# A hybrid attention and expert layer: the first norm's gain and bias applied after the turn, the residual rows made later, the first pair's small products moved

## The chip, the core and the metric

The kernel runs on one core of a Trainium2 chip. Five engines work side by side, each through its own queue in order: PE (TensorE, matrix products), DVE (VectorE), ACT (ScalarE), POOL (GpSimd) and SP (SyncE, which here only issues DMAs). Data move between memory and the core's SBUF by 16 DMA engines. The metric is the device time of one execution in microseconds, as the median of several runs.

## What is computed

One layer on 512 tokens of width 1024, in float32: a layer norm, two kinds of attention from one input projection, an output projection with a residual, a second norm, 32 experts of which each token uses two, and a last norm.

```python
h = layer_norm(x, ln_emb_g, ln_emb_b)
proj = h @ w_in[l]
qa, ka, va, cq, ckv, kr = jnp.split(proj, IN_SPLITS, axis=-1)
...
mixed = jnp.concatenate([rms_norm(out_a, ...), rms_norm(out_b, ...)], -1) @ w_out[l]
h = layer_norm(DEEPNORM_ALPHA * h + mixed, ln_attn_g[l], ln_attn_b[l])
ffn = hierarchical_moe(h, ...)      # group, then top 2 of 8 experts; silu(t@gate)*(t@up) @ down
h = layer_norm(DEEPNORM_ALPHA * h + ffn, ln_ffn_g[l], ln_ffn_b[l])
```

So the first norm's result is used twice: turned (features on partitions) as the operand of `w_in`, and as rows (tokens on partitions) in the residual sum before the second norm.

## The kernel before

Tokens are in four tiles of 128. **First norm.** For each tile `load_x` brings `xt`; `ln_stats` forms mean and 1/deviation on DVE (with a power on POOL); `layer_norm` writes the row tile `z[t]` with two DVE instructions for each half of 512, from the gain and bias `lng` and `lnb` that stand broadcast on all partitions. PE turns `z[t]` in eight 128x128 pieces into the PSUM tile `ptr`, and `split` makes of it `hth` (rounded, on ACT) and `htl` (the rest, on DVE), since every product is made of three: high by high, low by high, high by low.

**Projection.** `w_in` is worked through in four chunks of at most 512 columns. `chunk_load` loads four pieces `wf` of 512 KB each (four buffers) and splits them into `wh` (ACT) and `wl` (POOL in the first chunk, DVE afterwards). `chunk` makes the products of each token tile in one of four PSUM accumulators (two `pwo`, two `pmm`, in turn). The first and second chunks give the low-rank tokens `cqt`, which are turned and split to `cth` and `ctl`; the third gives the key and value (`kar`, `ka`, `kall`), the fourth the queries of the windowed attention, which go through `rope` (`rp`, then `cqt`, `qa`) and are turned. In these parts a scheduler decides the order on each engine from its own forecast, so the order of the code isn't that of the queues.

**Later parts.** The low-rank projections and both attentions follow. From `manual_schedule` on (L1075) the order of the code is the order of each queue. There the last token tile's output projection is made in halves (`wout_h`, `wout_l`, `add_z`), with the routing of the last two tiles (a and b) between: `logits`, `biased`, `route` (a chain of some ten small DVE instructions), `count` (PE), `place` and `sel0_` (DVE), and the second norm's rows (`norm_gain`, `norm_bias`, `scaled`, `gain`, `shift`). `gather` collects the rows of the first two experts into `xT0`.

**Experts.** 32 experts go in 16 pairs: `gates` (product with the gate and up weights, tile `p_gu`), `gated` (`hid` on ACT and DVE, turned to `hidT`), `down`, `leave_rows` (weighting on DVE, scatter by POOL). Six slots of weights form a ring: a pair's `load_next` issues, on SP's queue, the weight loads of the pair three later as its gates let go of the slots. The first two slots' gate weights are in three pieces: for j = 0 and 1, for j = 2 and 3, for j = 4 to 7 (j counts the 128-row blocks of the token width). Rows of later experts come by `fetch`, an indirect DMA from POOL into `xg`, after `places_rows` has turned 16 small products into row numbers. Pair 0 differs: its gates are cut after j = 1 for these 16 products (`run_pair`), and `residual(0)` scales its rows before the weighting.

## Time and profile before

| | |
|---|---|
| median of three runs | 592.02 us (591.60 to 595.59) |
| the profiled execution's own time | 591.33 us |
| its span | 589.5 us |
| PE busy | 523.4 us, 89% of the span |
| DVE, ACT, POOL busy | 322.6, 222.1, 99.9 us |
| moved by DMA | 141.76 MB |

The span is what the profiler saw from the first instruction to the last; the execution's own time is 1.8 us longer. Busy shares are means over very different stages, so the prediction reads windows of the span, and inside them the order of time.

### The profile page before, as it was taken

Reading aid. Unit: us, or ns where it says so; the run is one execution under the profiler, and the core shown is the slowest. Engines: PE = TensorE matmul, PEld = TensorE weight load, DVE = VectorE, ACT = ScalarE, POOL = GpSimd, SP = SyncE. Lnnn points to the kernel's source line nnn. Section 1 sums busy time; section 2 is a strip of 40 time slices with the busy share of each in tenths; the row PEclk is TensorE's granted clock in tenths of the full one; section 3 lists DMA queues with packets and bytes.
Section 4 is the critical chain, followed back from the end, with each engine's and each line's share of the span. In section 5 each row is a group of like instructions: output and inputs, shape, how many; then the busy total and the mean of one; then the engine's idle time right before and its main releaser. Section 6 shows DMA issues by size and latency. Waiting matters only on the chain. (4 is left out here: it accounts for less than half of the span.)

```text
span 589.5 us, 8004 instructions
## 1 busy us (share of the span) xinstructions
PE 523.4 (89%) x2756; PEld 331.8 (56%) x2757; DVE 322.6 (55%) x882; ACT 222.1 (38%) x477; POOL 99.9 (17%) x141
## 2 busy tenths in 40 slices
PE   2899999999898999999998899999998699979860
PEld 1688898789766777677777444343433234323230
DVE  4946463775688757947768734434524222202177
ACT  2256451564597738856731312111111111101032
POOL 1700221311100000213200201123111101000051
PEclk9999999999899999999999989999999889989985
DMA  8983310221201005991266799999999999999663
GB/s 279 280 290 81 102 43 0 59 81 42 85 16 58 1 1 212 289 367 39 66 258 259 280 391 410 420 415 415 411 417 400 421 418 391 412 420 416 264 267 142
DMA packets 46268, 141.76 MB, mean 240 GB/s; under 512 B 12380, under 2 KB 19420, under 8 KB 37009
## 3 DMA queue, kind: packets, MB, share of 16 engines
q1 hardware_dynamic: 40608, 131.06, 58.5%
q0 software_dynamic: 4464, 8.06, 3.6%
q10 hardware_dynamic: 1152, 2.10, 0.9%
q8 instruction: 23, 0.38, 0.3%
q14 instruction: 21, 0.16, 0.1%
HBM read 133.14 MB, written 16.25 MB: 253 GB/s over the span
## 5 line engine op out<-in xcount | busy, mean ns | idle before, releaser
L1243 PE MATMUL p_gu<-w_gu,xT 128*64 128x512 f32 x512 | 125.0, 613 | 15.0 <-DMA w_gu<-in_w_gu 14.1
L1243 PEld LDWEIGHTS p_gu<-w_gu,xT 128*64 128x64 f32 x512 | 39.6, 141 | 95.6 <-issue 70.0
L1247 ACT ACTIVATE hid<-p_gu 128x256 f32<-128x256 f32 x16 | 6.1, 384 | 176.0 <-PE p_gu L1243 163.9
L1248 DVE TENSOR_TENSOR hid<-hid,p_gu 128x256 f32<-128x256 f32 x16 | 6.7, 421 | 113.9 <-ACT hid L1247 113.8
L1263 PE MATMUL p_y<-w_dn,hidT 128*64 128x512 f32 x256 | 59.9, 611 | 1.0 <-issue 0.6
L1276 DVE SCALAR_TENSOR_TENSOR xg<-p_y,wsl,xg 128x512 f32<-128x512 f32 x30 | 22.5, 751 | 28.4 <-PE p_y L1263 26.5
L1263 PEld LDWEIGHTS p_y<-w_dn,hidT 128*64 128x64 f32 x256 | 17.5, 140 | 31.4 <-issue 29.3
L604 PE MATMUL ptr<-cst,pr 128*128 128x128 f32 x208 | 33.3, 278 | 1.9 <-ACT pr L562 1.4
L1034 POOL DMA_INDIRECT xg<-norm_rows,tok x16 | 16.5, 1032 | 104.5 <-PE p_y L1263 16.8
L1269 POOL DMA_INDIRECT moe_rows<-xg,idx x15 | 15.6, 1039 | 95.0 <-DVE xg L1276 69.6
L604 PEld LDWEIGHTS ptr<-cst,pr 128*128 128x128 f32 x208 | 24.9, 145 | 9.5 <-ACT pr L562 3.2
L577 ACT ACTIVATE pr<-pmm,bnm 128x512 f32<-128x512 f32 x32 | 22.0, 689 | 10.6 <-DVE bnm L574 9.7
L574 DVE TENSOR_REDUCE bnm<-pmm 128x1 f32<-128x512 f32 x32 | 21.9, 687 | 5.3 <-PE pmm L215 4.8
L215 PE MATMUL pmm<-wh,htl 128*128 128x512 f32 (+1 forms) x64 | 24.0, 374 | 0.0
L213 PE MATMUL pmm<-wh,hth 128*128 128x512 f32 (+1 forms) x64 | 23.8, 372 | 0.0
L214 PE MATMUL pmm<-wl,hth 128*128 128x512 f32 (+1 forms) x64 | 23.5, 368 | 0.0
L562 ACT ACTIVATE pr<-pr,rc 128x512 f32<-128x512 f32 (+2 forms) x32 | 20.6, 645 | 4.1 <-DVE rc L560 3.9
L590 DVE CUSTOM_DVE_ANT_0 sm<-pmm,mask,nsink 128x256 f32<-128x256 f32 (+1 forms) x32 | 17.4, 545 | 7.6 <-PE pmm L587 6.5
L215 PE MATMUL pwo<-wh,htl 128*128 128x512 f32 (+1 forms) x56 | 20.7, 370 | 0.0
L214 PE MATMUL pwo<-wl,hth 128*128 128x512 f32 (+1 forms) x56 | 20.5, 367 | 0.0
L213 PE MATMUL pwo<-wh,hth 128*128 128x512 f32 (+1 forms) x56 | 20.5, 367 | 0.0
L1232 ACT ACTIVATE xg<-xg,of 128x1024 f32<-128x1024 f32 x15 | 17.2, 1149 | 8.5 <-PE p_x L1228 7.8
(349 smaller groups left out, 1161.6 us busy)
## 6 DMA issues: line engine op xcount, KB each, us to landing
w_gu<-in_w_gu SPq DMA_DIRECT2D x52, 1024.0 KB
w_dn<-in_w_dn SPq DMA_DIRECT2D x20, 1024.0 KB
w_gu<-in_w_gu SPq DMA_DIRECT2D x24, 512.0 KB
w_dn<-in_w_dn SPq DMA_DIRECT2D x24, 512.0 KB
wf<-in_w_in SPq DMA_DIRECT2D x12, 512.0 KB
moe_rows<-zr SPq DMA_DIRECT2D x8, 512.0 KB
rows<-moe_rows SPq DMA_DIRECT2D x8, 512.0 KB
wf<-in_w_q_b SPq DMA_DIRECT2D x12, 192.0 KB
```

The source lines that it names most:

```text
L213: PE.matmul(ps, ah, bh, start=first, stop=False)
L214: PE.matmul(ps, ah, bl, start=False, stop=False)
L215: PE.matmul(ps, al, bh, start=False, stop=last)
L562: SC.mul(pr[:, :n], pr[:, :n], rc)
L574: V.tensor_reduce(nm, sp, AX.X, ALU.max, negate=True)
L577: exps_.append(SC.activation(pr[:, :S], sp, AF.Exp, bias=nm, accum_out=den).ins)
L590: V.tensor_tensor_reduce(sm[:, :nk], sp[:, :nk], mask[:, mo:mo + nk], 1.0, nsink[:, h:h + 1], ALU.add, ALU.min, nm)
L604: PE.transpose(pt[:, k * P:(k + 1) * P], pr[:, k * P:(k + 1) * P], ident)
L1232: SC.mul(pl["xg"], pl["xg"], pl["of"])
L1243: PE.matmul(pg[64 * i:64 * i + 64], xT[:, j, 64 * i:64 * i + 64], ws[i][0][j], start=(j == 0), stop=(j == 7))
L1263: r = PE.matmul(py[64 * i:64 * i + 64, :], hT[:, j, 64 * i:64 * i + 64], ws[i][1][n][:, j], start=(j == 0), stop=(j == 1))
L1276: V.scalar_tensor_tensor(y, py, pl["wsl"], y, ALU.mult, ALU.add)
```

## The change

1. **First norm.** The four broadcast loads of `lng` and `lnb` (256 KB each) go, and so do the 16 DVE instructions of `layer_norm`. `cst` (identity and tables) is loaded first and by ACT's queue, with a new small tile `geT` that holds gain and bias with features on partitions (given by the host). ACT now writes z = x * rs + nb in two instructions for each tile; the turned pieces get gain and bias as per-partition numbers on their way from `ptr` into a new SBUF tile `hf`, six by DVE and two by ACT for each token tile; `split` reads `hf`. The first chunk's `wl` is split by DVE like the others.
2. **Residual rows.** `z` now lacks gain and bias. They are loaded, broadcast, into two of the fourth chunk's `wf` buffers (512 KB each), and 16 DVE instructions of 128x512 apply them, in the code inside the fourth chunk's loop.
3. **Last routing.** `logits(a)` is made inside `wout_h(0)`, `route(a)` goes ahead of `place(0)`, `count(a)` behind `turn(b, 1)`, and some norm steps change places.
4. **First pair.** The gates of pair 0 run without a cut in the order j = 4 to 7, 0 to 3; the 16 small products go into `gated`'s two gaps (`rows_mm`), so that the fetches, `residual(0)` and `places_mm` come after them; `weights(1..3)` is called ahead of the gates, and the fetches of pair 1's rows are issued in the order 1, 0, 2, 3.

DVE from the program's first loads on, before (z_64 and z_65 are the rows of the first two token tiles):

```order
L192 BN_STATS ln_st<-xt 128x6 x2
L194 BN_AGGR ln_mv<-ln_st 128x2
L181 TENSOR_SCALAR rsq_t<-ln_mv 128x1
L203 SCALAR_TENSOR_TENSOR z_64<-xt,ln_mv,lng 128x512
L204 SCALAR_TENSOR_TENSOR z_64<-z_64,ln_rs,lnb 128x512
L203 SCALAR_TENSOR_TENSOR z_64<-xt,ln_mv,lng 128x512
L348 CAST identr<-cst 128x128
L204 SCALAR_TENSOR_TENSOR z_64<-z_64,ln_rs,lnb 128x512
L209 TENSOR_TENSOR htl<-ptr,hth 128x4x128
L192 BN_STATS ln_st<-xt 128x6 x2
L209 TENSOR_TENSOR htl<-ptr,hth 128x4x128
```

and now:

```order
L191 BN_STATS ln_st<-xt 128x6
L351 CAST identr<-cst 128x128
L191 BN_STATS ln_st<-xt 128x6
L193 BN_AGGR ln_mv<-ln_st 128x2
L180 TENSOR_SCALAR rsq_t<-ln_mv 128x1
L248 SCALAR_TENSOR_TENSOR ln_nb_156<-ln_mv,ln_rs 128x1
L191 BN_STATS ln_st<-xt 128x6
L201 TENSOR_TENSOR wl<-wf,wh 128x1024
L191 BN_STATS ln_st<-xt 128x6
L262 TENSOR_SCALAR hf<-ptr,geT 128x128 x4
L193 BN_AGGR ln_mv<-ln_st 128x2
L262 TENSOR_SCALAR hf<-ptr,geT 128x128
```

The writing of `z` is gone from DVE, and the weight splits and the `hf` instructions have come between the statistics and the first `htl`.

DVE where the third chunk ends and the fourth begins, before (rp_990 belongs to the first query tile):

```order
L424 TENSOR_TENSOR ka_922<-kar,ka_922 128x256
L431 CAST kall<-ptr 128x2x128 x2
L321 TENSOR_TENSOR rp_990<-pwo,ctq 128x512
L329 TENSOR_TENSOR rp_991<-pwo,stq 128x8x32 x2
L209 TENSOR_TENSOR qa_996<-cqt,qa_996 128x8x64
L321 TENSOR_TENSOR rp_1037<-pmm,ctq 128x512
```

and now (wf is the tile that holds the gain, then the bias):

```order
L427 TENSOR_TENSOR ka_958<-kar,ka_958 128x256
L447 TENSOR_TENSOR z_64<-z_64,wf 128x512 x2
L447 TENSOR_TENSOR z_65<-z_65,wf 128x512 x2
L447 TENSOR_TENSOR z_66<-z_66,wf 128x512 x2
L447 TENSOR_TENSOR z_67<-z_67,wf 128x512 x2
L434 CAST kall<-ptr 128x2x128
L448 TENSOR_TENSOR z_64<-z_64,wf 128x512 x2
L448 TENSOR_TENSOR z_65<-z_65,wf 128x512 x2
L448 TENSOR_TENSOR z_66<-z_66,wf 128x512 x2
L448 TENSOR_TENSOR z_67<-z_67,wf 128x512
L434 CAST kall<-ptr 128x2x128
L448 TENSOR_TENSOR z_67<-z_67,wf 128x512
```

The scheduler has put all 16 row instructions in one block ahead of the first query tile's `rope`, around the last two key casts.

PE in pair 0, before, from the second half of the gates for j = 1 on (w_gu_2878 and w_gu_2884 are the two experts' pieces for j = 0 and 1; psd takes the small products):

```order
L1243 MATMUL p_gu<-w_gu_2878,xT 64x512
L1243 MATMUL p_gu<-w_gu_2884,xT 64x512
L1368 MATMUL psd<-cmb_73,sel_2562 128x2 x2
L1368 MATMUL psd<-cmb_73,sel 128x2 x2
L1368 MATMUL psd<-cmb_74,sel 128x2 x4
L1368 MATMUL psd<-cmb_75,sel 128x2 x4
L1368 MATMUL psd<-cmb_76,sel 128x2 x4
L1243 MATMUL p_gu<-w_gu_2880,xT 64x512
```

and now, from the last gates on (the pieces for j = 2 and 3; those for j = 4 to 7, then 0 and 1, stand ahead of them):

```order
L1254 MATMUL p_gu<-w_gu_2942,xT 64x512
L1254 MATMUL p_gu<-w_gu_2936,xT 64x512
L1254 MATMUL p_gu<-w_gu_2942,xT 64x512
L1391 MATMUL psd<-cmb_73,sel_2618 128x2 x2
L1391 MATMUL psd<-cmb_73,sel 128x2 x2
L1391 MATMUL psd<-cmb_74,sel 128x2 x4
L1263 MATMUL p_t<-cst,hid 128x128 x2
L1391 MATMUL psd<-cmb_75,sel 128x2 x4
L1391 MATMUL psd<-cmb_76,sel 128x2 x4
L1007 MATMUL p_i<-cmb_73,sel_2618 128x6 x2
```

The 16 small products have left the middle of the gates and stand on both sides of the turn of `hid` (`p_t`), with `places_mm` (`p_i`) behind.

```diff
@@ -137,12 +137,11 @@
             t = pl.tile([P, n], F32, name=name)
             SY.dma_start(out=t, in_=src.partition_broadcast(P))
             return t
+
+        geT = cp.tile([P, 2, NK], F32, name="geT")
+        SC.dma_start(out=cst, in_=A["cst"][:, :C_KEEP])
+        SC.dma_start(out=geT, in_=A["ge_T"])
         load_x(0)
-        lg, lb = [lp.tile([P, D], F32, name=nm) for nm in ("lng", "lnb")]
-        for n in range(2):
-            for dst, nm in ((lg, "ln_emb_g"), (lb, "ln_emb_b")):
-                SY.dma_start(out=dst[:, 512 * n:512 * n + 512], in_=A[nm][512 * n:512 * n + 512].partition_broadcast(P))
-        SY.dma_start(out=cst, in_=A["cst"][:, :C_KEEP])
 
         nch = [-1]
 
@@ -162,7 +161,7 @@
                                  in_=A["w_in"][0, 256 * q:256 * q + 256, c0:c0 + w]
                                  .rearrange("(k p) f -> p k f", p=P))
                     o += w
-                split(wf[:, :, :n], wh[:, :, :n], wl[:, :, :n], PO if nch[0] == 0 else V)
+                split(wf[:, :, :n], wh[:, :, :n], wl[:, :, :n])
                 hs.append((wh, wl))
             return n, hs
 
@@ -196,13 +195,6 @@
             rsqrt(rs, mv[:, 1:2], 1.0, eps)
             return mv, rs
 
-        def layer_norm(src, dst, g, b):
-            mv, rs = ln_stats(src)
-            for i in range(2):
-                sl = slice(512 * i, 512 * i + 512)
-                V.scalar_tensor_tensor(dst[:, sl], src[:, sl], mv[:, 0:1], g[:, sl], ALU.subtract, ALU.mult)
-                V.scalar_tensor_tensor(dst[:, sl], dst[:, sl], rs, b[:, sl], ALU.mult, ALU.add)
-
         def split(src, hi, lo, ev=None):
 
             r = SC.copy(hi, src).ins
@@ -250,15 +242,26 @@
                 chunks.append(chunk_load([(768, 512)]))
             elif t + 1 < NT:
                 load_x(t + 1)
-            layer_norm(xs[t], z[t], lg, lb)
+
+            mv, rs = ln_stats(xs[t])
+            nb = small.tile([P, 1], F32, name="ln_nb0")
+            V.scalar_tensor_tensor(nb, mv[:, 0:1], -1.0, rs, ALU.mult, ALU.mult)
             for kk in range(2):
+                sl = slice(512 * kk, 512 * kk + 512)
+                SC.activation(z[t][:, sl], xs[t][:, sl], AF.Identity, scale=rs, bias=nb)
                 pt = ptr()
                 for k in range(4):
                     PE.transpose(pt[:, k * P:(k + 1) * P],
                                  z[t][:, (4 * kk + k) * P:(4 * kk + k + 1) * P], ident)
-                pv = pt.rearrange("p (a b) -> p a b", a=4)
+                hf = lp.tile([P, 4, P], F32, name="hf", bufs=2)
+                for k in range(4):
+                    g_, b_ = [geT[:, i, 4 * kk + k:4 * kk + k + 1] for i in range(2)]
+                    if kk and k % 2:
+                        SC.activation(hf[:, k], pt[:, k * P:(k + 1) * P], AF.Identity, scale=g_, bias=b_)
+                    else:
+                        V.tensor_scalar(hf[:, k], pt[:, k * P:(k + 1) * P], g_, b_, ALU.mult, ALU.add)
                 o = (slice(None), slice(4 * kk, 4 * kk + 4), slice(t * P, (t + 1) * P))
-                split(pv, hth[o], htl[o])
+                split(hf, hth[o], htl[o])
         lnst.close()
 
 
@@ -431,10 +434,18 @@
             V.tensor_copy(kal[:, :, t * P:(t + 1) * P],
                           f32v(pt[:, 256:512]).rearrange("p (a b) -> p a b", a=2))
         qc = chunk_load([(0, 512)])
+        lgb = [wp.tile([P, 2, 512], F32, name="wf", bufs=4) for _ in range(2)]
+        for dst, nm in zip(lgb, ("ln_emb_g", "ln_emb_b")):
+            SY.dma_start(out=dst, in_=A[nm].rearrange("(a b) -> a b", a=2).partition_broadcast(P))
         for i in range(2 * S // P):
             SY.dma_start(out=yd[i * P:(i + 1) * P, :].rearrange("p (a b) -> p a b", a=4),
                          in_=zr.unsqueeze(1).to_broadcast([P, 4, 256]))
         for t, pp in chunk(qc):
+            for i in range(2):
+
+                zt = z[t][:, 512 * i:512 * i + 512]
+                V.tensor_tensor(zt, zt, lgb[0][:, i], ALU.mult)
+                V.tensor_tensor(zt, zt, lgb[1][:, i], ALU.add)
             qr_ = scr0.tile([P, H * 64], F32, name="cqt").rearrange("p (a b) -> p a b", a=H)
             rope(qr_, pp.rearrange("p (a b) -> p a b", a=H), tabq, t, H, 32, scr)
             q2 = scr1.tile([P, H, 2, 64], F32R, name="qa2")
@@ -1142,16 +1153,17 @@
                 sp.append(psd("sum"))
                 for q in range(4):
                     PE.matmul(sp[0][:, 0:1], sq[:, q], iota1[:, 0:1], start=(q == 0), stop=(q == 3))
+            if k in (1, 2):
+                logits(a, k - 1)
         p0 = wout_h(0, sumsq)
         norm_gain(a, 0)
         rr = small.tile([P, 1], F32, name="rr")
         rsqrt(rr, sp[0][:, 0:1], ALPHA ** 2 / 512, ALPHA ** 2 * RMS_EPS)
         norm_bias(a, 0)
-        logits(a, 0)
-        logits(a, 1)
         wout_l(0, p0)
         count(0)
         biased(a)
+        steps(route(a))
         place(0)
         sel0_(0)
         add_z(0, p0)
@@ -1159,11 +1171,10 @@
         p1_ = wout_h(1)
         count(1)
         norm_tiles(b)
+        norm_gain(a, 1)
+        place(1)
         wout_l(1, p1_)
-        steps(route(a))
-        place(1)
         turn(b, 0)
-        count(a)
         add_z(1, p1_)
         als.close()
         wk.append(pool(top, "work2", bufs=2))
@@ -1175,17 +1186,17 @@
         rsqrt(rs, mv[:, 1:2], 1.0, LN_EPS / ALPHA ** 2)
         negmean(b)
         turn(b, 1)
-        place(a)
+        count(a)
         sel0_(1)
-        sel0_(a)
+        norm_bias(a, 1)
         logits(b, 0)
         logits(b, 1)
         offset(b)
         for i in (1, 0):
             scaled(b, i)
-        norm_gain(a, 1)
+        place(a)
+        sel0_(a)
         biased(b)
-        norm_bias(a, 1)
         for i in range(2):
             keep(a, i)
         gather(0, range(2))
@@ -1237,10 +1248,10 @@
         def new_gates(tag="ptr"):
             return ps.tile([P, 2 * FF], F32, name="p_gu", tag=tag, bufs=2)
 
-        def gates(pg, xT, ws, j0, j1):
-            for j in range(j0, j1):
+        def gates(pg, xT, ws, order=range(NK)):
+            for n, j in enumerate(order):
                 for i in range(2):
-                    PE.matmul(pg[64 * i:64 * i + 64], xT[:, j, 64 * i:64 * i + 64], ws[i][0][j], start=(j == 0), stop=(j == 7))
+                    PE.matmul(pg[64 * i:64 * i + 64], xT[:, j, 64 * i:64 * i + 64], ws[i][0][j], start=(n == 0), stop=(n == NK - 1))
 
         def gated(pg, meanwhile=lambda i: None):
             hid = wk[0].tile([P, FF], F32, name="hid", bufs=1)
@@ -1360,22 +1371,7 @@
 
         def run_pair(p, xT, meanwhile):
             pg = new_gates()
-            if p == 0:
-                gates(pg, xT, ws[p], 0, 2)
-                pi = psd("places")
-                for t in range(NT):
-                    for u in range(4):
-                        PE.matmul(pi[:, 2 * u:2 * u + 2], (sel0[t], sels[1][t])[u // 2][:, P * (u % 2):P * (u % 2) + P],
-                                  cmb[t][:, 2 * u:2 * u + 2, 0], start=(t == 0 and u == 0), stop=(t == NT - 1 and u == 3))
-                for g in range(2):
-                    for u, pl in enumerate(places_rows(pi[:, 4 * g:4 * g + 4], 2, 2, 1)):
-                        plc[2 * g + u] = pl
-                        fetch(2 * g + u, pl)
-                for t in range(1, NT):
-                    weights(t)
-                gates(pg, xT, ws[p], 2, 8)
-            else:
-                gates(pg, xT, ws[p], 0, 8)
+            gates(pg, xT, ws[p], (4, 5, 6, 7, 0, 1, 2, 3) if p == 0 else range(NK))
             load_next(p)
             r = leave_rows(gated(pg, meanwhile), ws[p], plc[p])
             load_next_dn(p)
@@ -1385,16 +1381,34 @@
 
             SC.mul(plc[p]["xg"], plc[p]["xg"], plc[p]["of"])
 
+        pis = []
+
+        def rows_mm(t0, t1):
+            if t0 == 0:
+                pis.append(psd("places"))
+            for t in range(t0, t1):
+                for u in range(4):
+                    PE.matmul(pis[0][:, 2 * u:2 * u + 2], (sel0[t], sels[1][t])[u // 2][:, P * (u % 2):P * (u % 2) + P],
+                              cmb[t][:, 2 * u:2 * u + 2, 0], start=(t == 0 and u == 0), stop=(t == NT - 1 and u == 3))
+
         xT = xT0
+        for t in range(1, NT):
+            weights(t)
         for p in range(NP - 1):
             nx = new_xT()
 
             def meanwhile(i):
                 if p == 0:
-                    if i == 0:
+
+                    rows_mm(2 * i, 2 * i + 2)
+                    if i == 1:
+                        for g in range(2):
+                            for u, pl in enumerate(places_rows(pis[0][:, 4 * g:4 * g + 4], 2, 2, 1)):
+                                plc[2 * g + u] = pl
+                            for q in ((1, 0), (2, 3))[g]:
+                                fetch(q, plc[q])
                         residual(0)
-                    else:
-                        pi = psd("places")
+                        pi = ps.tile([P, 512], F32, name="p_i", tag="ptr", bufs=2)
                         places_mm(pi, sel0, [weights_of(u) for u in range(2)], range(NT))
                         places_weights(pi, [plc[0], plc[1]], 6, 3, 1)
                     return
```

## Rows read from the trace of the kernel before

**Rows 1.** The page: engines' busy time; the costliest group (busy, mean ns, idle before).

```profile
PE 523.4 (89%) x2756; PEld 331.8 (56%) x2757; DVE 322.6 (55%) x882; ACT 222.1 (38%) x477; POOL 99.9 (17%) x141
...
L1243 PE MATMUL p_gu<-w_gu,xT 128*64 128x512 f32 x512 | 125.0, 613 | 15.0 <-DMA w_gu<-in_w_gu 14.1
```

**Rows 2.** Windows of the span, columns as in the first line.

```profile
core 0: us, PE busy (x) PEld busy (x) DVE busy (x) ACT busy (x) POOL busy (x), PEclk, DMA share, GB/s
3.00:7.00 4.00, 0.00 (x0) 0.00 (x0) 1.75 (x4) 0.00 (x0) 0.55 (x1) 1.00 0.86 207
13.00:20.00 7.00, 4.39 (x10) 2.60 (x11) 6.96 (x9) 3.81 (x5) 6.74 (x4) 1.00 0.88 280
25.00:40.00 15.00, 15.00 (x77) 12.41 (x76) 9.27 (x19) 4.67 (x11) 1.85 (x2) 1.00 1.06 377
80.00:100.00 20.00, 20.00 (x109) 17.06 (x108) 11.21 (x28) 6.85 (x13) 3.57 (x5) 1.00 0.00 1
329.00:339.00 10.00, 8.24 (x50) 4.49 (x49) 7.32 (x42) 2.23 (x4) 4.26 (x4) 0.98 0.69 222
```

**Rows 3.** Timeline of the first 25 us: start, length, engine, line, idle before.

```profile
8.01 0.75 DVE L203 SCALAR_TENSOR_TENSOR z<-xt,ln_mv,lng 128x512 f32<-128x512 f32 x1 [2.32 <-DMA lng<-in_ln_emb_g]
...
13.23 1.22 PE L385 MATMUL pwo<-wh,hth 128*128 128x512 f32 x2 [0.76 <-ACT wh L208]
...
16.77 5.61 DVE L204 SCALAR_TENSOR_TENSOR z<-z,ln_rs,lnb 128x512 f32<-128x512 f32 x2
17.18 1.04 ACT L208 CAST wh<-wf 128x1024 fp32r<-128x1024 f32 x1 [0.30 <-DMA wf<-in_w_in]
...
19.75 1.09 PE L257 MATMUL ptr<-cst,z 128*128 128x128 f32 x4 [2.10 <-DVE z L204]
...
24.91 1.09 PE L385 MATMUL pwo<-wl,hth 128*128 128x512 f32 x4
```

**Rows 4.** Groups of one form in the first 60 us: busy, mean ns.

```profile
L209 POOL TENSOR_TENSOR wl<-wf,wh 128x1024 fp32r<-128x1024 f32 x4 | 10.4, 2628 | 6.9 <-ACT wh L208 6.9
L204 DVE SCALAR_TENSOR_TENSOR z<-z,ln_rs,lnb 128x512 f32<-128x512 f32 x8 | 9.9, 1269 | 0.1
...
L209 DVE TENSOR_TENSOR wl<-wf,wh 128x1024 fp32r<-128x1024 f32 x4 | 4.9, 1222 | 1.1 <-ACT wh L208 1.1
...
L306 DVE TENSOR_SCALAR stq<-sn 128x128 f32<-128x128 f32 x2 | 0.4, 219 | 0.0
```

**Rows 5.** Timeline of the fourth chunk: DVE as it begins, PE behind its end.

```profile
89.27 0.41 DVE L431 CAST kall<-ptr 128x256 fp32r<-128x256 f32 x1
...
94.47 0.42 DVE L431 CAST kall<-ptr 128x256 fp32r<-128x256 f32 x1 [4.79 <-ACT kall L429]
95.30 0.69 DVE L321 TENSOR_TENSOR rp<-pwo,ctq 128x512 f32<-128x512 f32 x1 [0.40 <-PE pwo L215]
95.90 0.75 DVE L329 TENSOR_TENSOR rp<-pwo,stq 128x256 f32<-128x256 f32 x2
...
107.43 0.39 PE L213 MATMUL pwo<-w2h,cth 128*128 128x512 f32 x1
```

**Rows 6.** Timeline of the last routing and of pair 0's gates.

```profile
305.38 1.05 PE L1144 MATMUL psd<-cst,asq 128*128 128x1 f32 x8 [0.28 <-ACT asq L1135]
...
317.62 0.81 ACT L1114 ACTIVATE z<-z,ln_nb,ln_rs 128x512 f32<-128x512 f32 x1 [0.90 <-DVE ln_nb L1119]
...
322.74 0.68 DVE L1122 TENSOR_TENSOR z<-z,lngb 128x512 f32<-128x512 f32 x1
...
326.17 0.69 DVE L1208 COPY xT<-p_g 128x512 f32<-128x512 f32 x1 [1.54 <-PE p_g L1109]
...
326.92 1.94 PE L1243 MATMUL p_gu<-w_gu,xT 128*64 128x512 f32 x8 [0.78 <-DVE gn L892]
...
328.88 9.21 SPq L692 DMA_DIRECT2D w_gu<-in_w_gu  x6
...
330.66 5.37 PE L1243 MATMUL p_gu<-w_gu,xT 128*64 128x512 f32 x24
```

More of the change, by code (lines that the diff above doesn't have):

```diff
@@ L1487, in build @@
         with tc.issue_after(last):
-            gates(pg, xT, ws[p], 0, 8)
+            gates(pg, xT, ws[p])
         hT = gated(pg)
```

3 lines of the change are left out of this document (2 added, 1 removed).

## The prediction

> **What bounds the kernel now.** Read the page first [rows 1]: PE is busy 89% of the span, and its only large idle group is 15.0 us ahead of the expert gates, 14.1 of it for the transfer of their weights. So two things in turn set the time. Until the experts it is PE: in the windows [rows 2] it is busy 15.00 of 15 us from 25 on, and 20.00 of 20 up to 100. In the experts it is the weight transfers: at first they run ahead of PE, and in the later pairs PE waits for them, so that what counts there is how early and how densely the DMA engines work. The transfers that fill the ring start when PE lets go of buffers in the last output projection. A shift of PE before that therefore shifts the whole flood and the end with it; a gain of PE after that counts only for as much as the DMA engines had stood idle. In the window 329 to 339 they were used at 0.69, so 3.1 us were idle.
>
> Then the start [rows 3]. PE's first product comes at 13.23 and it waits again until 19.75, when the second token tile's z arrives. Three things made it late: the wait of 2.32 us for the broadcast gain, the two L204 that took 5.61 us together while POOL split weights beside them, and weight pieces of which the last was cast at 17.18, right behind its landing. The products there are slow: a pair takes 1.22 us at 13.23, four take 1.09 us at 24.91. That is the lower level of the clock against the upper one, although the clock column of the windows prints 1.00 throughout [rows 2].
>
> **First norm.** Gone from DVE are 16 instructions of about 0.75 us [rows 3], 12.0, and the lengthening of two of them, 5.61 - 1.50 = 4.1: together 16.1 us. New on DVE: the 24 hf instructions of 128x128. The same operation from SBUF takes 0.219 [rows 4]; they read PSUM, where a cast of twice the columns takes 0.41 [rows 5]. So 5.3 to 9.8 us; I take 0.25 each, 6.0, since most of such a short instruction is not its columns. The four weight splits come over from POOL, where they took 10.4 us, at 1.22 on DVE [rows 4]: 4.9. DVE is left with 16.1 - 6.0 - 4.9 = 5.2 us less. ACT gets eight z instructions, 0.81 each by the same form late in the program [rows 6], 6.5 us, and eight hf at about 0.3, 2.4 us. It was busy only 3.81 of 7 us in 13 to 20 [rows 2], but its queue is in order, so hth of a tile now stands behind weight casts and z.
>
> On the path: 1 MB of broadcast disappears from ahead of the weight pieces. By the rate in 3 to 7, 207 GB/s, that is 5.1 us; by the 377 of the later window, 2.8 [rows 2]. The last piece then comes at 12 to 14 instead of 17.2. DVE had finished its statistics at 8.01 - 2.32 = 5.69, so 1/deviation, with the small power on POOL, is there at some 6.3 (an estimate). Then ACT: one weight cast, two z of 0.81, two casts of 1.04 and hth, half as wide, at about 0.6 lead to 6.3 + 1.0 + 1.6 + 2.1 + 0.6, about 11.6; PE's turn and four hf, about 3 us, lie beside these casts. So the first product starts near 11.6 instead of 13.23. The second tile's z waits on ACT for one more weight cast, two hf, the second hth and gaps for DVE (two splits of 1.22 and htl), and ends near 16.3; before, PE got it at 19.75. That gives 3.4 us less 0.6 for four pieces that are now turned earlier in PE's queue, 2.8. If PE, dense from about 13.5, also gets its upper clock sooner than the shift alone says, products of about 4 us are made at half the length: up to 4.7. If the clock rises no sooner than at 24.9, nearly all is lost: 0.7. I take **3.2**.
>
> [...]
>
> **Residual rows.** 16 instructions of 128x512 at 0.68 [rows 6] are 10.9 us on DVE, in one block between the two key casts. DVE had 4.79 us idle there [rows 5], and the casts are wanted by nobody soon. So the first query's rope starts not at 95.30 but at about 95.30 + 10.9 - 4.8 - 0.6 = 100.8 at most, and nearer 100 as back-to-back instructions overlap a little. A rope is about 1.4 us on DVE [rows 5], so three of them, caught up behind each other, end at 104.2 to 105, and the fourth, whose products PE ends at about 107.4 [rows 5], is on time or 0.5 late. The products of the chunk have four accumulators, so PE needs none of this back before the chunk's end; the turn of the first queries, which stood in the chunk's middle, now stands behind its last product in PE's queue, at about 107. PE: **0**, up to 1 if the first w2l of the next projection is late. The loads come when two of the four buffers are split, at about 84 and 87, on DMA engines with a share of 0.00 in 80 to 100 [rows 2]. At 207 GB/s each takes 2.5 us and some 2 to start: 88.5 and 91.5, against first uses at 89.7 and 95. Queued behind them on SP are the last key/value weight piece and the query weights, which have until after 107.
>
> **Routing and first pair.** On PE: logits(a) now fill a wait of 0.28 us for the squares [rows 6]; the gates of pair 0 start with the half of xT that ACT copies, not behind DVE's copy at 326.17 + 0.69 [rows 6], about 1.05 us sooner together, at 325.9; and the 16 products leave the middle (330.66 - 328.86 = 1.8 us). Without the cut they take 1.94 + 5.37 = 7.3 us, and end at 333.2 instead of 336.0: 2.8 us. But the flood sees less. SP issues the first piece's successor, 1 MB in two, when the gates for j = 0 and 1 are done, which was at 328.88; these are now the last but one, done at 325.9 + 5.4 = 331.2. So the engines dry up 1 MB, 2.5 us, earlier, and the rest follow by 333.2, where the six issues had taken until 338.1 [rows 6]. Of the 3.1 us of idle DMA about 2.6 stay. The fetches now come 2.5 us later, behind 4 MB of issued weights, at 377 GB/s 11 us (an estimate): rows land near 345 to 347, and pair 1's gates start some 2 us later than before. The flood has more than 2 MB of issued loads then, so nothing is late by it. Together **0.6** us sooner at the end, from 0 to 2.8.
>
> **Sum.** 591.33 - 3.2 - 0 - 0.6 = 587.5 for the profiled execution; the median is 0.69 above it, so **588.2**.
>
> **Rivals.** (1) All of pair 0's gain counts: if the dry time of the DMA engines is set by the end of the gates and not by their first piece, another 2.2 us: **586.0**. For it: most of the six loads issued from 328.88 on waited for later gates [rows 6]. Against: the first 1 MB is what bridged the gap. (2) The first norm gains nothing: the chain through ACT (z, hf, hth in one queue) costs what the transfer gives, or the clock rises at the old time: 591.33 - 0.7 - 0.6 + 0.7 = **590.7** to 591.4. For it: DVE was full in 13 to 20 (6.96 of 7) and gets four splits; against: 5.2 us less on DVE in all. (3) Slower: the gain and bias land late, and the block of 16 holds up the ropes. The turn of the first queries at about 107.2 needs the block to be over three ropes and a split, 4.9 us, sooner, at 102.3; each us beyond that is one of PE's. If the second load lands not at 91.5 but at 103, its eight additions of 5.4 us end at 108.4, a loss of 6.1 us: **594.3**. It outweighs the gain of 3.8 only when the block ends after 106.1. Against it: nothing else is on the DMA engines. (4) What was moved doesn't count because the scheduler has ordered the attention otherwise; 2 us either way, inside the range.
>
> **How the numbers follow.** Forecast 0.50, (1) 0.15, (2) 0.21, (3) 0.09, others 0.05. The range takes in (1), (2) and the clock's upper case together with part of (1) below (591.33 - 4.7 - 2.8 + 0.7 = 584.5), and (3) above: 584.0 to 594.0. 1% is 5.9 us, about what a measurement of this kernel can tell from no change: faster than 586.1 are half of (1) and the forecast with the clock's full gain, 0.20; slower than 597.9 only a worse (3), 0.05; within, 0.75.
>
> **What would show it.** Right: first product near 11.6, second tile's pieces near 16.5, PE without a wait from there; w_out of the last tile and the first weights of the flood some 3 us sooner in the trace; rope of the first queries near 100 and PE busy through 107; idle DMA of 2 to 3 us around 330. Wrong: PE waits for hth or htl between 12 and 25 as before, four products in 1.09 us no sooner than 24.9; PE idle at 107; a flood that starts sooner but ends no sooner, where PE or the last pair's chain would have become the bound.

## The result, and the profile after

The changed kernel takes 597.38 us (median of 22, 593.90 to 601.63) and the kernel before, run with it, 593.40 (median of 22); the ratio is 1.0072 with a 95% interval of 1.0045 to 1.0098. It is slower by about 4.3 us, where 3.8 less were forecast. The profiled execution took 595.91 us with a span of 594.3. The interval excludes 1; the ratio itself is under the 1% that was called no change.

The page of the kernel after, engines and costliest group, against [rows 1]: PE has 6.9 us more to do with as many products, and its gates take 629 ns each instead of 613.

```profile
PE 530.3 (89%) x2756; PEld 337.0 (57%) x2757; DVE 329.5 (55%) x914; ACT 231.0 (39%) x493; POOL 88.9 (15%) x137
...
L1254 PE MATMUL p_gu<-w_gu,xT 128*64 128x512 f32 x512 | 128.1, 629 | 12.5 <-DMA w_gu<-in_w_gu 11.9
```

As many products that take longer mean a lower clock: the mean granted clock is 0.955 in this profile and 0.970 in that of before.

The first 25 us of after, in order of time, against [rows 3]:

```profile
9.78 1.05 ACT L200 CAST wh<-wf 128x1024 fp32r<-128x1024 f32 x1 [0.47 <-DMA wf<-in_w_in]
9.85 1.35 DVE L262 TENSOR_SCALAR hf<-ptr,geT 128x128 f32<-128x128 f32 x4
...
11.12 1.04 ACT L200 CAST wh<-wf 128x1024 fp32r<-128x1024 f32 x1 [0.29 <-DMA wf<-in_w_in]
...
12.07 0.61 ACT L200 CAST hth<-hf 128x512 fp32r<-128x512 f32 x1
...
12.74 1.22 PE L388 MATMUL pwo<-wh,hth 128*128 128x512 f32 x2 [2.11 <-ACT hth L200]
...
18.15 1.24 PE L254 MATMUL ptr<-cst,z 128*128 128x128 f32 x8
...
20.65 2.00 PE L388 MATMUL pwo<-wl,hth 128*128 128x512 f32 x8
```

The first product comes 0.5 us sooner, the second tile's pieces 1.6 sooner and without a wait; and eight products take 2.00 us from 20.65 on, where that length for four (1.09) came at 24.91. What this gives further on is read from PE's turns of the third chunk's keys. The kernel before, in the profile of [rows 1] and in a second one, called `b2`:

```profile
L427 PE MATMUL ptr<-identr,ka x16: 220/224/232, 80.4 to 93.8; 128*128 128x128 f32 x16
```

```profile
L427 PE MATMUL ptr<-identr,ka x16: 220/224/232, 79.5 to 92.9; 128*128 128x128 f32 x16
```

After, and `u34`, which has the same first norm and is told of below:

```profile
L430 PE MATMUL ptr<-identr,ka x16: 220/224/232, 77.0 to 90.4; 128*128 128x128 f32 x16
```

```profile
L430 PE MATMUL ptr<-identr,ka x16: 220/224/232, 78.3 to 91.7; 128*128 128x128 f32 x16
```

After is 3.4 us ahead of the first profile of the kernel before. But the start differs from one execution to the next: of the eleven profiles with the new first norm after is furthest ahead (1.8 to 3.4, middle 2.15), and eight further profiles with the old one stand at 0.2 behind to 1.5 ahead (middle 1.0).

The fourth chunk in after: DVE's block, and PE behind the chunk's end, against [rows 5].

```profile
85.86 4.89 DVE L447 TENSOR_TENSOR z<-z,wf 128x512 f32<-128x512 f32 x8
...
96.16 0.68 DVE L324 TENSOR_TENSOR rp<-pwo,ctq 128x512 f32<-128x512 f32 x1
...
111.01 0.54 PE L456 MATMUL ptr<-identr,qa 128*128 128x128 f32 x4 [0.34 <-ACT q L458]
112.34 0.85 PE L456 MATMUL ptr<-identr,qa 128*128 128x128 f32 x8 [0.79 <-DVE qa L201]
113.73 1.54 PE L479 MATMUL ptr<-cst,ktok 128*96 128x128 f32 x8 [0.54 <-DVE q L458]
```

The rope starts at 96.16 against 95.30, so 4.3 us behind PE's earlier timetable, and PE waits three times, 1.67 us in all. Before, it waited 1.0 us there, by the list of PE's waits from 96 to 120:

```profile
PE ptr L468 <- DVE q L447: 0.5, 1, 0.5
PE ptr L445 <- DVE q L447: 0.5, 1, 0.5
```

From 114.1 to 117.5 PE then has the lower clock in after, a granted 0.50. At 120 us 1.05 of the 3.4 us are left; later stretches give back some, so that it is 2.0 to 2.2 between 240 and 304. All ten profiles that have the row instructions show these waits. Four of them (after, `nat`, `early`, `resdve_fill`) also show the lower clock behind them and lose 2.4 us here; the six without it lose 0.7.

Now the last output projection. Windows of after and of the kernel before, columns as in [rows 2]; `b2` and `b3` are the unchanged kernel before, profiled again.

After:

```profile
290.00:313.00 23.00, 22.63 (x129) 17.80 (x128) 16.81 (x73) 7.66 (x23) 1.83 (x4) 0.85 0.53 183
```

The kernel before, second profile (`b2`):

```profile
290.00:313.00 23.00, 22.54 (x150) 17.92 (x150) 16.06 (x69) 7.99 (x23) 1.83 (x4) 1.00 0.53 183
```

PE is as busy in both but makes 129 products instead of 150: from 305.3 to 312.1 the granted clock is 0.50 in after, and the mean of `b2` from 290 to 313 is 1.00. So the 2 us are gone before the flood of expert weights begins: its first load leaves at 314.46, against 313.26 (`b2` 312.51, `b3` 313.21).

Then pairs 0 and 1 in after, in order of time, against [rows 6]:

```profile
325.48 7.09 PE L1254 MATMUL p_gu<-w_gu,xT 128*64 128x512 f32 x32
...
336.79 1.27 POOL L1045 DMA_INDIRECT xg<-norm_rows,tok  x1 [19.61 <-DVE idt L1018]
...
345.85 1.59 PE L1239 MATMUL p_x<-cst,xg 128*128 128x128 f32 x8 [4.82 <-DMA xg<-norm_rows,tok]
...
347.76 1.15 ACT L1382 ACTIVATE xg<-xg,of 128x1024 f32<-128x1024 f32 x1 [14.74 <-DMA xg<-norm_rows,tok]
348.82 0.56 ACT L1240 COPY xT<-p_x 128x512 f32<-128x512 f32 x1
...
349.44 8.87 PE L1254 MATMUL p_gu<-w_gu,xT 128*64 128x512 f32 x32 [0.50 <-ACT xT L1240]
...
354.90 4.71 SPq L703 DMA_DIRECT2D w_gu<-in_w_gu  x4
```

Pair 0's gates are as short as forecast, 7.09 us, and the window from 329 to 339 has a DMA share of 0.82 instead of 0.69 [rows 2]:

```profile
329.00:339.00 10.00, 9.91 (x54) 5.03 (x52) 7.19 (x43) 0.50 (x2) 1.91 (x2) 0.85 0.82 282
```

So far the first pair gains. But the fetches begin at 336.79, their rows come at 345.7, and PE, with pair 0's work done, waits 4.82 us for them. ACT's copy of the turned rows stands behind `residual(0)` (the ACTIVATE at 347.76), which waits for pair 0's own rows. The granted clock is 0.50 from 346.2 to 353.1, the gates of pair 1 take 8.87 us, and the next weights are asked for at 354.90. Before, the same gates and the same loads, in order of time:

```profile
345.98 7.09 PE L1243 MATMUL p_gu<-w_gu,xT 128*64 128x512 f32 x32
...
349.66 4.71 SPq L692 DMA_DIRECT2D w_gu<-in_w_gu  x4
```

So they come 5.2 us later than in this profile. The two others of the kernel before stand closer, as a longer fall of the clock to 0.50 (338.0 to 344.8 in `b2`, 338.7 to 345.5 in `b3`, 338.7 to 342.1 in the first) goes with a longer `down` of pair 0 there: 6.53 us in `b3`, 5.11 in the first. `b3`:

```profile
339.68 6.53 PE L1263 MATMUL p_y<-w_dn,hidT 128*64 128x512 f32 x16
...
347.95 7.09 PE L1243 MATMUL p_gu<-w_gu,xT 128*64 128x512 f32 x32
...
351.63 4.87 SPq L692 DMA_DIRECT2D w_gu<-in_w_gu  x4
```

The windows from 345 to 365, after first and then before, show what it costs: the DMA share falls from 1.00 to 0.82, 3.6 us of 20.

```profile
345.00:365.00 20.00, 18.26 (x86) 9.15 (x88) 8.09 (x26) 4.79 (x6) 1.01 (x1) 0.83 0.82 306
```

```profile
345.00:365.00 20.00, 19.62 (x105) 8.38 (x105) 8.62 (x29) 3.61 (x5) 3.15 (x3) 1.00 1.00 400
```

### The profile page after: what moved, and what is told of

It is laid out like the page before. It is cut to its first block, busy times and chain, and to the rows that moved or that the text cites. A ratio compares the mean times of both kernels' runs of the same rounds, so it can differ in the third digit from the quotient of the medians.

```text
span 594.3 us, 8046 instructions
## 1 busy us (share of the span) xinstructions
PE 530.3 (89%) x2756; PEld 337.0 (57%) x2757; DVE 329.5 (55%) x914; ACT 231.0 (39%) x493; POOL 88.9 (15%) x137
## 5 line engine op out<-in xcount | busy, mean ns | idle before, releaser
L1254 PE MATMUL p_gu<-w_gu,xT 128*64 128x512 f32 x512 | 128.1, 629 | 12.5 <-DMA w_gu<-in_w_gu 11.9
L1254 PEld LDWEIGHTS p_gu<-w_gu,xT 128*64 128x64 f32 x512 | 41.8, 145 | 94.8 <-issue 71.7
L1045 POOL DMA_INDIRECT xg<-norm_rows,tok x16 | 16.5, 1029 | 107.3 <-issue 32.4
L1239 PE MATMUL p_x<-cst,xg 128*128 128x128 f32 x120 | 19.2, 285 | 4.8 <-DMA xg<-norm_rows,tok 4.8
L1239 PEld LDWEIGHTS p_x<-cst,xg 128*128 128x128 f32 x120 | 13.7, 143 | 17.0 <-issue 13.8
```

The costliest lines, as they stand in the source:

```text
L1239: PE.transpose(pt[:, k], pl["xg"][:, P * (4 * j2 + k):P * (4 * j2 + k) + P], ident)
L1254: PE.matmul(pg[64 * i:64 * i + 64], xT[:, j, 64 * i:64 * i + 64], ws[i][0][j], start=(n == 0), stop=(n == NK - 1))
```

## The experiments

Ratios are to the kernel before on the same chip, with the 95% interval. The clock is the median of the mean granted clocks of the executions, and in brackets that of the kernel before. The expectations give their theories letters; the text says each in words. The rows come from five chips, so ratios of different groups are compared with care: `u34`, `p3`, `p4` and `u4` from one, `u34_nr`, `nat` and `early` from a second, `fill5`, `p3a` and `p3b` from a third, `resdve` and `resdve_fill` from a fourth, the last two from a fifth.

| kernel | ratio | interval | clock |
|---|---|---|---|
| u34: first norm and residual rows alone | 0.9946 | 0.9917 to 0.9975 | 0.970 (0.965) |
| u34_nr: first norm alone | 0.9923 | 0.9893 to 0.9954 | 0.972 (0.965) |
| p3: last routing alone | 1.0048 | 1.0019 to 1.0078 | 0.961 (0.965) |
| p4: first pair alone | 1.0062 | 1.0038 to 1.0086 | 0.959 (0.965) |
| u4: all but the first pair | 1.0035 | 1.0005 to 1.0064 | 0.964 (0.965) |
| nat | 1.0042 | 1.0007 to 1.0077 | 0.958 (0.965) |
| early | 1.0006 | 0.9975 to 1.0038 | 0.961 (0.965) |
| fill5 | 1.0073 | 1.0041 to 1.0105 | 0.961 (0.967) |
| resdve | 1.0064 | 1.0036 to 1.0091 | 0.957 (0.966) |
| resdve_fill | 1.0022 | 0.9988 to 1.0056 | 0.964 (0.966) |
| p3a | 1.0021 | 0.9996 to 1.0046 | 0.964 (0.967) |
| p3b | 1.0010 | 0.9976 to 1.0043 | 0.966 (0.967) |
| p3_fill | 1.0040 | 1.0009 to 1.0071 | 0.963 (0.967) |
| u34_fill | 1.0004 | 0.9974 to 1.0033 | 0.966 (0.967) |

And what each one's trace shows, in us: the flood's first load, then the start of pair 1's gates and the next weight load counted from it, the time from these gates' start to `hid`, and the idle time of the DMA engines from 345 to 375 (one less the share, summed over windows of 1 us).

| kernel | first load | gates of pair 1 | their length | next load | DMA idle | span |
|---|---|---|---|---|---|---|
| before | 313.3 | +32.7 | 7.2 | +36.4 | 0.5 | 589.5 |
| b2 | 312.5 | +34.7 | 7.2 | +38.4 | 1.0 | 590.3 |
| b3 | 313.2 | +34.7 | 7.2 | +38.4 | 1.3 | 592.7 |
| after | 314.5 | +35.0 | 8.9 | +40.4 | 3.8 | 594.3 |
| u34 | 314.9 | +31.9 | 7.2 | +35.6 | 0.6 | 591.4 |
| p3 | 315.7 | +34.4 | 8.7 | +39.7 | 3.1 | 594.9 |
| p4 | 317.6 | +35.1 | 9.5 | +41.1 | 4.3 | 598.3 |
| nat | 315.5 | +35.0 | 9.1 | +40.6 | 5.9 | 595.7 |
| early | 314.5 | +29.9 | 7.2 | +33.6 | 0.1 | 592.3 |
| fill5 | 314.1 | +35.2 | 8.7 | +40.4 | 4.1 | 594.1 |
| resdve | 317.4 | +34.7 | 8.9 | +40.2 | 3.5 | 597.1 |
| resdve_fill | 315.2 | +32.9 | 7.2 | +36.5 | 0.7 | 591.0 |
| p3_fill | 315.8 | +33.6 | 7.2 | +37.3 | 0.9 | 593.0 |
| u34_fill | 315.7 | +32.4 | 7.2 | +36.1 | 0.4 | 592.6 |

One profile is one execution: three of the same kernel before span 589.5 to 592.7 us, so the spans of this table don't rank the kernels; the ratios do.

**Which part costs.** `u4` has all but the first pair's new order; `u34` also has the old routing; `p4` and `p3` are the kernel before with one part each. In short:

```diff
 # u34, from the kernel after (u4: the second piece only)
-            if k in (1, 2):
-                logits(a, k - 1)
...
-            gates(pg, xT, ws[p], (4, 5, 6, 7, 0, 1, 2, 3) if p == 0 else range(NK))
+            if p == 0:
+                gates(pg, xT, ws[p], range(0, 2))
...
 # p3, from the kernel before
+        steps(route(a))
         place(0)
```

> The changed kernel with pair 0 as it was before (gates cut after j = 1, the 16 products there, fetches at once, natural order). Theory A (the late fetch of pair 1's rows makes PE wait 4.8 us, run at the lower clock and let its slots go 5.2 us late, which leaves the DMA engines idle for 3.6 us near 354): that idle is gone, the time falls by 3.5 to 4.5 us against the changed kernel, to a ratio of 0.997 to 1.001 of the kernel before. Theory B (the last routing in its new order lets the clock fall during the output projection, so the weight flood starts 1.2 us later): the loss stays, 1.004 to 1.007. Theory C (the block of 16 row instructions costs 2.4 us around 110 to 117): no change of its own here.

> The changed kernel with the last routing and pair 0 as they were before, so only the first norm and the residual rows are changed. Theories A and B: what is left is the gain seen up to 300 us, 2.0 us, so 0.996 to 0.998. If the gain up to 300 us does not carry to the end: 1.000. Theory C alone (the loss sits in the block of rows): 1.000 to 1.004.

> The kernel before with pair 0's new order alone. Theory A: PE waits for pair 1's rows by 4 to 5 us, DMA engines idle some 3 us near 355, end 2.5 to 4.5 us later: 1.004 to 1.008. Theory B: no loss, 0.997 to 1.000.

> The kernel before with the last routing's new order alone. Theory A: no loss, the flood starts within 0.5 us of before, 0.999 to 1.001. Theory B: the clock falls while the output projection's second half runs, the flood starts about 3 us later than the rest of the trace says, 1.003 to 1.006.

The first norm with the residual rows alone is faster than both kernels, 0.9946, and of 593.4 us that is 3.2; the routing alone costs 2.8, the first pair alone 3.7. The product of the three ratios is 1.0056, within the interval of the whole. So by the time parts 1 and 2 do what was forecast, and parts 3 and 4 cost, each by itself. The one profile of `u34` doesn't show its gain: it has the low clock of the last output projection as well (307.0 to 313.8; 0.87 as the mean from 290 to 313), and its first load leaves at 314.9.

**The residual rows.** `u34_nr` is `u34` without the loads of gain and bias and the 16 instructions; its residual sum therefore lacks them.

```diff
-                V.tensor_tensor(zt, zt, lgb[0][:, i], ALU.mult)
-                V.tensor_tensor(zt, zt, lgb[1][:, i], ALU.add)
```

> Only the first norm changed, and the residual rows left out (no loads of gain and bias, no 16 instructions, so the residual is taken without them). Theory C (the block of rows costs 2.4 us around 110 to 117): the whole 3.4 us of the first stage is seen at 300 us, ratio 0.988 to 0.992. If the block costs nothing: as with the rows, 0.993 to 0.997.

By these two the rows cost some 0.2%, with intervals that overlap and on two chips, so the times don't show whether they cost anything. Of the 2.35 us that after lost behind the fourth chunk 1.1 is given back by 240 us, and in `u34`, without the lower clock there, 0.7 is lost.

**The order in pair 0.** `nat` runs pair 0's gates uncut in the order 0 to 7, with the late fetch; `early` keeps the order 4 to 7, 0 to 3, but cuts the gates after two for the small products and the fetches.

```diff
 # nat, from the kernel after
-            gates(pg, xT, ws[p], (4, 5, 6, 7, 0, 1, 2, 3) if p == 0 else range(NK))
+            gates(pg, xT, ws[p], range(NK))
 # early, from the kernel after
+                gates(pg, xT, ws[p], (4, 5))
...
+                gates(pg, xT, ws[p], (6, 7, 0, 1, 2, 3))
```

> The changed kernel with pair 0's gates in natural order 0 to 7, uncut, the rest of pair 0 as changed (fetches late). Theory A (late fetches cost the time): as the changed kernel, 1.005 to 1.009, PE waits 4 to 5 us for pair 1's rows, DMA idle about 4 us between 345 and 375. Theory D (the order 4 to 7, 0 to 3 costs it, since the first weight piece is let go later): 2 to 2.5 us better, 1.001 to 1.004, with that idle below 2 us.

> The changed kernel with pair 0's gates in the order 4 to 7, 0 to 3, but cut after two of them for the 16 products, with the fetches at once and in the order 0 to 3 as before. Theory A: PE's wait for pair 1's rows falls to about 2 us, DMA idle between 345 and 375 below 1 us, 0.997 to 1.002. Theory D: as the changed kernel, 1.005 to 1.008.

The late fetch costs: with the fetches back in their old place the ratio falls from 1.0072 to 1.0006, and the intervals don't overlap. That the order of the gates costs isn't shown: `nat` (1.0042) can't be told from the changed kernel, nor from `early`, and its trace has the same wait for the rows, 3.91 us, with 5.9 us of idle DMA. In `early`, in order of time, the loads that refill the ring leave at 335.21, 4 us later than in after (330.87), and pair 1's gates are yet made at full clock (1.00 from 345 to 365):

```profile
335.21 4.28 SPq L703 DMA_DIRECT2D w_gu<-in_w_gu  x6
...
344.42 7.09 PE L1255 MATMUL p_gu<-w_gu,xT 128*64 128x512 f32 x32
```

So what `early` loses around 335 (6.0 us of idle DMA from 325 to 345, against 2.0 in after) it has back from 345 on (0.1 against 3.8).

**Why pair 1 is late.** Two causes offered themselves: PE's idle 4.82 us, behind which the clock is low, and ACT's copy behind `residual(0)`. `fill5` puts five products of 128x512 that nobody reads behind pair 0's `down`; `resdve` scales the rows of `residual(0)` on DVE; `resdve_fill` does both.

```diff
 # fill5, from the kernel after
+                for _ in range(5):
+                    PE.matmul(pf, ident, xT0[:, 0:4], start=True, stop=True)
 # resdve, from the kernel after
-            SC.mul(plc[p]["xg"], plc[p]["xg"], plc[p]["of"])
+            V.tensor_scalar(plc[p]["xg"], plc[p]["xg"], plc[p]["of"], None, ALU.mult)
```

> The changed kernel with five products of 128x512 into an unread PSUM tile behind pair 0's last product, so that PE works while it would wait for pair 1's rows (nothing else is changed; they are extra work). Theory F (the late rows cost little by themselves; PE's idle wait makes the clock fall, and pair 1's gates at half clock let the slots go late): the gates of pair 1 take 7.1 us instead of 8.9, the next weights are issued about 36.5 to 37.5 us behind the flood's first load instead of 40.4, DMA idle between 345 and 375 falls from 3.8 to about 1 us, ratio 1.000 to 1.003. Theory A' (the landing of the rows itself is what costs): as the changed kernel or slower, 1.006 to 1.009.

> The changed kernel with the scaling of pair 0's rows (residual(0)) on DVE, not in ACT's queue. Theory H (ACT's copy of pair 1's turned rows stands behind this scaling, which waits for pair 0's rows, now fetched second): pair 1's gates start about 33 us behind the flood's first load instead of 35.0, the next weights follow at 37 to 38.5 instead of 40.4, DMA idle between 345 and 375 falls from 3.8 to 2 us or less, ratio 1.002 to 1.005. Theory A' (only the landing of pair 1's own rows counts): as the changed kernel, 1.006 to 1.009.

> The same with the five extra products of the filled kernel behind pair 0, so that both of pair 1's delays are met: the queue on ACT and the clock. Theory F with H: gates of pair 1 at 33 us and 7.1 us long, the next weights at 36.5 to 37.5 us, idle below 1 us, ratio 0.999 to 1.002. Theory H alone: no more than the kernel without the filling, 1.002 to 1.005.

Neither alone helps by the ratios, both together seem to: 1.0072 as it is, 1.0073 and 1.0064, and 1.0022. The intervals of the last overlap those of the others (0.9988 to 1.0056, against 1.0045 to 1.0098 and 1.0036 to 1.0091), so the times alone don't show it; one trace of each shows what happens in pair 1. PE in `fill5`, in order of time (L1429 are the five added products, in two records each):

```profile
340.60 4.56 PE L1429 MATMUL p_f<-xT,cst 128*128 128x512 f32 x10
345.65 1.09 PE L1239 MATMUL p_x<-cst,xg 128*128 128x128 f32 x8 [0.49 <-DMA xg<-norm_rows,tok]
...
349.31 8.61 PE L1254 MATMUL p_gu<-w_gu,xT 128*64 128x512 f32 x32 [1.78 <-ACT xT L1240]
```

The wait for the rows is filled, but then PE waits for ACT's copy, and the clock is low again, from 349.0 to 352.4 (0.57 as the mean from 349 to 353). In `resdve` the copy comes at once, but PE has waited 4.85:

```profile
348.85 1.86 PE L1239 MATMUL p_x<-cst,xg 128*128 128x128 f32 x8 [4.85 <-DMA xg<-norm_rows,tok]
...
352.14 8.87 PE L1254 MATMUL p_gu<-w_gu,xT 128*64 128x512 f32 x32
```

In `resdve_fill`, timeline and then window, neither wait is there, the clock is 1.00 and the DMA share 0.99:

```profile
346.27 1.09 PE L1239 MATMUL p_x<-cst,xg 128*128 128x128 f32 x8
346.96 0.59 ACT L1240 COPY xT<-p_x 128x512 f32<-128x512 f32 x1 [13.19 <-PE p_x L1239]
...
348.08 7.10 PE L1254 MATMUL p_gu<-w_gu,xT 128*64 128x512 f32 x32
```

```profile
345.00:365.00 20.00, 19.61 (x103) 8.60 (x104) 11.01 (x34) 3.75 (x5) 2.71 (x3) 1.00 0.99 383
```

In after the granted clock was 0.50 from 346.2 to 353.1, behind 4.82 us of waiting. Not every wait did it: in all 20 profiles the gates of pair 1 had the lower clock where PE had waited 2.3 to 6.8 us for rows and copy (eight profiles, `fill5` with 0.49 and 1.78 the least), and none of it where it had waited 2.05 us (`u34`), 1.86 (`u4`) or not at all (ten).

**The routing.** `p3a` takes of `p3` only `logits(a)` inside `wout_h`, `p3b` all the rest; `p3_fill` is `p3` with three unread products behind pair 0's `down`.

```diff
 # p3a, from the kernel before
+            if k in (1, 2):
+                logits(a, k - 1)
...
-        logits(a, 0)
-        logits(a, 1)
 # p3_fill, from p3
+                for _ in range(3):
+                    PE.matmul(pf, ident, xT0[:, 0:4], start=True, stop=True)
```

> The kernel before with only the products logits(a) moved into the first half of the output projection. If part 3's loss (1.0048) comes from the small products in the middle of that half (theory B): 1.003 to 1.006. Theory G (PE reaches the gates earlier while the row writes and fetches keep to the flood, so PE waits longer and its clock falls in pair 1): 0.999 to 1.002 here, since this alone moves the gates by 0.3 us.

> The kernel before with the last routing's other moves only (route, place, count, norm steps), logits(a) where they were. Theory G: 1.003 to 1.006, gates of pair 0 about 12 us behind the flood's first load instead of 13.7, a wait of 2 to 3 us for pair 1's rows and in most executions the half clock in its gates. Theory B: 0.999 to 1.001.

> The kernel before with the last routing's new order, and three extra products of 128x512 into an unread PSUM tile behind pair 0's last product. Theory G with F (the new routing costs time by a wait of PE for pair 1's rows and the half clock that follows in pair 1's gates): that wait is filled, gates of pair 1 take 7.1 us, next weights at 36 to 37 us behind the flood's first load instead of 39.7, ratio 0.998 to 1.002. Theory B (it is lost ahead of the flood): as without the filling, 1.003 to 1.007.

Neither half can be told from no change, and together they are 0.5%. In their traces it is `p3a` that waits 2.54 us for pair 1's rows and has the lower clock in these gates, and `p3b` that has no such wait, the opposite of what theory G expected. In the timeline of `p3` PE waits for pair 1's rows as well:

```profile
348.23 1.09 PE L1228 MATMUL p_x<-cst,xg 128*128 128x128 f32 x8 [3.07 <-DMA xg<-norm_rows,tok]
```

`p3_fill` mends pair 1 (gates 7.2 instead of 8.7, idle DMA 0.9 instead of 3.1), yet its ratio is 1.0040 against 1.0048. So pair 1 explains at most a part; what else the routing costs is not settled. Put into the best kernel, the same three products bring nothing:

> First norm and residual rows changed, routing and pair 0 as before, with the same three extra products. Theory F: its own wait of 2 us for pair 1's rows let the clock fall in some executions only (its profile shows none), so a little is left to gain: 0.991 to 0.995. If the filling only adds work: 0.995 to 0.999.

It is 1.0004 against 0.9946 for `u34`, worse than either expectation. `u34` does have a wait there, with the clock at 1.00 behind it:

```profile
344.93 1.09 PE L1239 MATMUL p_x<-cst,xg 128*128 128x128 f32 x8 [2.05 <-DMA xg<-norm_rows,tok]
```

The three products take 2.84 us, most of which lie in that wait, so their work doesn't explain 0.6%. The intervals just touch (0.9975 and 0.9974) and the chips differ; why a kernel so close to `u34` shows no gain stays open, and with it how much of the 0.9946 another measurement would find.

**The low clock in the last output projection.** `u4b`, `b2`, `b3` and `p4b` are further profiles of kernels already told of (`u4`, twice the kernel before, `p4`), with nothing edited.

> The kernel before again, for a second look at its clock. Theory E (the fall of the clock in the last output projection belongs to the execution and not to the new order): one look can show it here too; where it falls, the first load of the flood is issued 1.5 to 3.5 us later than 313.3 and the end moves with it. Theory B: the clock prints 1.00 from 290 to 313 as in the first look.

> The changed kernel with pair 0 as before, a second look (the first profile was of its fastest execution, 590.84 us). Theory G: an execution of 595 to 599 us shows pair 1's gates at half clock behind a wait for its rows, the next weights about 39 to 40 us behind the flood's first load, not 36.6. Theory B: the time is lost ahead of the flood.

> The kernel before, a third look at its clock ahead of the flood. Theory E (the fall of the clock in the last output projection belongs to the execution): it can show here as it did with the kernel that has only pair 0's order changed, whose instructions are the same up to the gates; then the first load of the flood comes at 315 to 318 instead of 312.5 to 313.3, and the time is 3 to 4 us above the two first looks. If it belongs to the kernel: no fall, 312.5 to 313.5.

> The kernel before with pair 0's new order alone, a second look. Theory E: the first load of the flood may come at 312.5 to 314 here, and the time then is 3 us below its first look's 600.2, 596 to 597.5. If it belongs to the kernel: again the half clock between 305 and 317 and a first load at 317 to 318.

Windows from 310 to 316: `b3`, then `p4b`, whose instructions up to 326 us are those of the kernel before.

```profile
310.00:316.00 6.00, 4.48 (x29) 3.47 (x29) 5.37 (x18) 0.59 (x1) 0.00 (x0) 1.00 0.31 76
```

```profile
310.00:316.00 6.00, 6.00 (x19) 4.18 (x18) 3.74 (x14) 0.00 (x0) 0.00 (x0) 0.50 0.00 0
```

Three profiles of the kernel before show no fall between 290 and 316; two of `p4` show it at 309.7 to 316.5 and 309.5 to 316.3. So the new routing, which `p4` lacks, isn't needed for it. Two profiles against three are too few to say that it belongs to the kernel and not to the execution, and it does move within one kernel: `u4` had it at 306.7 to 310.1, `u4b` at 317.0 to 323.9 (means from 305 to 325: 0.91 and 0.83). PE has no wait over 0.28 us in the 10 us ahead of it, in `p4b` as in `b3`. Why the one falls and the other doesn't stays open.

## Why the prediction was wrong

**First norm: about right, with luck.** 3.2 were forecast, and 3.4 stand in the profile of after at 75 to 94; but that is the largest of eleven, the others have 1.8 to 3.2, so the typical gain at the start is smaller than forecast. The first product came later than thought (12.74, not 11.6): ACT's casts of the weight pieces, counted there without a wait, began 0.5 us later and waited 0.47 and 0.29 us for their transfers, and `hth` stood behind the third of them. `hf` was ready at 11.20 and held nobody up there, though it too was mis-sized: it took about 0.40 us each on DVE and not 0.25, and 0.46 on ACT and not 0.3. The same operation from SBUF took 0.219 [rows 4], and a cast of twice the columns from PSUM 0.41 [rows 5], no longer than `hf` on DVE (0.36 to 0.41): so the columns alone don't give the size. Products of the short length came some 4 us sooner (eight in 2.00 us from 20.65, against four in 1.09 from 24.91) and made up for the late start. That the longer ones are the clock's lower level is my reading: the clock column prints 1.00 there in both kernels, but in after the six from 15.59 to 18.15 start 0.43 us apart, like the four from 308.73 to 310.44 at a granted 0.50, and the eight from 20.65 to 22.49 start 0.23 apart. The 3.2 supposes that products which start sooner are also fast sooner; no row of before shows that, it was my estimate, and what the eleven profiles showed in its place is a gain of 1.8 to 3.4. By the time, parts 1 and 2 together, forecast at -3.2, measured -3.2 (`u34`), though `u34_fill`, close to it, gave 1.0004.

**Residual rows: nearly right.** The block was over at 96.2 and not at 100. The second load, asked for at 83.10, was over by about 86, 2.9 us later (the DMA share is 0.82 in 84 to 85 and 0.06 in 86 to 87), where my estimate was 2.5 and some 2 to start. PE waited 1.67 us behind the chunk, 0.7 more than before, where 0 to 1 was said; the stretch at low clock that after has there on top was not foreseen. Timed by itself (`u34` against `u34_nr`) it is 0.2% or 1.4 us, which the intervals don't tell from 0 to 1.

**The step that failed** is the last of the third term: "The flood has more than 2 MB of issued loads then, so nothing is late by it." The rows landed when forecast (345.7 and 347.7, in 345 to 347), and pair 1's gates started 2.3 us later in the flood than in the profile predicted from, as forecast. But I carried these 2 us on as a plain shift. Behind the wait PE's clock was halved (0.50 against 1.00), the copy stood behind `residual(0)`, and the next loads came 4 us later in the flood (2 us against `b2` and `b3`), when the loads issued no longer bridged it: 3.8 us of idle DMA instead of 0.5 (1.0 and 1.3 in `b2` and `b3`). The four kernels above show both causes in their traces, and `early`, with the fetches at once, takes 0.7% back; `u4`, with all of pair 0 undone, takes 0.4%, with intervals that overlap. A second step failed as well, the sentence that w_out and the flood would start 3 us sooner: 2.0 us of gain were there up to 304 and went in the low clock of 305.3 to 312.1, whose cause is open.

Part 4, forecast with part 3 at -0.6, measured +3.7 alone, and part 3 measured +2.8, of which the wait for pair 1's rows explains at most a part. The profiled executions don't add up to these: the span of after is 4.8 us above the first profile of the kernel before, but 4.0 and 1.6 above `b2` and `b3`, and the idle DMA from 325 to 566 us, 12.5 us in after and 10.0 in the first profile, is 11.1 in `b3` and 12.6 in `early`. Of the rivals none named this; the third had the right sign, but its block ended at 96.2, far from the 106.1 that it needed.

## What to carry to other kernels

A step that is moved behind a weight flood can make the fetched rows late (here PE waited 4.82 us for them), and a late row is not only a shift: where PE then waits, its next products can be slow too (here 8.87 us instead of 7.09 for the same gates; behind 2.3 to 6.8 us of waiting, not behind 2.05), and whoever is queued behind a wait on ACT adds its own (here the copy, at 348.82 for rows that PE had turned by 347.44). So cost the wait together with the clock after it, and check on which engine the next operand's copy is queued. Time the parts of a compound change one by one: here the first two alone gave 0.9946, better than either kernel, though a near twin gave 1.0004. And profile the kernel before more than once: its three profiles differ by 2.0 us in where pair 1's next loads stand, half of what after seemed to lose there.
